# One unit of attention per head: both token tiles in one run of score products, 256-column value products, norm head by head

## The chip, the cores and the metric

The kernel runs on one core of one Trainium2 chip. The metric is the device time of one execution in microseconds, lower is better; the time shown is the median of 3 runs. Engines are called TensorE (PE, with its weight loads as PEld), VectorE (DVE), ScalarE (ACT), GpSimd (POOL) and SyncE (SP).

## The reference

Two layers of a decoder trunk over 256 tokens of 2048 features, in float32. The attention part that the change touches is, cut to its core:

```python
def _diff_attention(q, k, v, lam, rel_bias):          # 8 heads, 2 maps m, dk 64, dv 128
    ...
        s = jnp.einsum('bqhmd,bkhmd->bhmqk', qb, k) * scale + bias   # bias by distance
        s = jnp.where(dist >= 0, s, NEG)
        p = jax.nn.softmax(s, axis=-1)
        p = p[:, :, 0] - lam * p[:, :, 1]
        return jnp.einsum('bhqk,bkhd->bqhd', p, v)
...
    for l in range(2):
        h = _rmsnorm(x, attn_norm_g[l])
        q, k, v, gate_b, gate_c, conv_in = jnp.split(h @ w_in[l], splits, axis=-1)
        q, k = _rmsnorm(q, q_norm_g[l]), _rmsnorm(k, k_norm_g[l])    # per head and map
        attn = _rmsnorm(_diff_attention(q, k, v, lam, rel_bias), subln_g[l]) * (1 - lam_init)
        conv = gate_b * _short_conv(gate_c * conv_in, conv_w[l])
        x = x + jnp.concatenate([attn, conv], axis=-1) @ w_out[l]
        x = x + jnp.square(relu(_rmsnorm(x, mlp_norm_g[l]) @ w_up[l])) @ w_down[l]
```

## The kernel before

Tokens lie in two tiles of 128 (`t`). Every float32 operand of a large product is split in a high part, rounded to fp32r, and a low part, the rest; a product is the sum of three terms, high by high, high by low and low by high (`TERMS`). Weights come by DMA as `raw` tiles; ScalarE makes the high part `whi` (L289), VectorE the low part `wlo` (L290). There are three buffers each of `whi` and `wlo`, so the making of a weight tile waits until TensorE has read the one three before.

A layer's `mixer` runs, in this order on TensorE: q, k and v for heads 0 to 3 (`linear`, L354), q, k and v for heads 4 to 7, then four pairs of the gate columns gc and ci and four of gb (`linear_t`, L376: per weight tile eight products of 512 columns with `whi` and eight of 256 with `wlo`), then the output projection. `mlp` follows.

TensorE's instructions keep the order in which the code is written (`manual_schedule`); the other engines' are put in an order by the framework's scheduler. Everything that isn't the main stream of products is a generator in `work`; the main products call `work.tick()`, and a generator goes on when as many ticks have passed as it yielded last. A tick in `linear` comes after six products of 512 columns, in `linear_t` after four products. So attention is threaded into the product stream that follows: heads 0 to 3 run beside q, k and v of the second half, heads 4 to 7 beside the first gc and ci columns.

The attention of four heads (`attention`) is eight units, one for each token tile `t` and head `i`, each 4 ticks after the one before (`staggered(..., 4)`). A unit does:

- score products (L518): for each map `m`, three terms with 64 rows into a PSUM bank `sc`, of `W` = 128 columns for the first tile and 256 for the second; VectorE adds the bias and takes the row maximum in one instruction (L521), `nm` (L526) negates it, ScalarE takes the exponential with the row sums (L528), VectorE makes the reciprocal, the factor `c` and the mixed map `p` (L531 to L539); then `yield 9`
- one or two transposes of `p` (`ptp`, L544), split by ScalarE and VectorE into `pT` (L546, L547); then `yield 4`
- the value products (L554): three terms of 128 columns for each block `k` of keys, into the head's quarter of the bank `av`
- with the fourth head of a tile: `av` is copied out as `ao` (L562), squared head by head (L567), GpSimd makes the norm factor `af` in five small operations (L569, L396, L398, L572), VectorE multiplies (`an`, L574); then `yield 9`, four transposes (`atp`, L580) and the split into `cat` (L583, L584), which the output projection reads.

PSUM banks named by `bank` come from a rotation of three; `av` has one bank. The early loads of `w_up` (`uraw`) for the MLP stand in SyncE's queue among the loads of `w_in` and use memory that the attention's temporary tiles leave.

Of the kernel before, what the change touches and what calls it, by code (L numbers as in the profile page):

```python
# [21 lines left out]
NH = 8  # L22
DK = 64
# [5 lines left out]
CH = 512  # L29
# [8 lines left out]
TERMS = ((0, 0), (0, 1), (1, 0))  # L38
# [46 lines left out]
def staggered(pieces, apart):  # L85

    entries = [[i * apart, p] for i, p in enumerate(pieces)]
    while entries:
        for e in list(entries):
            if e[0] <= 0:  # L90
                try:
                    e[0] = max(1, next(e[1]))
                except StopIteration:
                    entries.remove(e)
                    continue
            e[0] -= 1
        if entries:
            yield 1
# [3 lines left out]
def trunk(ctx: ExitStack, tc: tile.TileContext, x, w_in, w_out, conv_w, q_norm_g, k_norm_g,  # L102
          lambda_q1, lambda_k1, lambda_q2, lambda_k2, subln_g, attn_norm_g, mlp_norm_g,
          w_up, w_down, rel_bias, selector, out):
    nc = tc.nc
# [45 lines left out]
    ident = const.tile([P, P], F32, tag="ident", name="ident")  # L151
# [41 lines left out]
    s_gain = const.tile([P, DEPTH], F32, tag="sg", name="s_gain")  # L193
    nlam = const.tile([P, DEPTH], F32, tag="nlam", name="nlam")
# [198 lines left out]
    def rstd_of(ss, n, name, shape):  # L393

        e = small.tile([P, shape], F32, tag="rs_e", name=f"{name}_e")
        nc.gpsimd.tensor_scalar(e, ss, 1.0 / n, EPS, op0=ALU.mult, op1=ALU.add)  # L396
        r = small.tile([P, shape], F32, tag="rs_r", name=f"{name}_r")
        nc.gpsimd.tensor_tensor(r, e, mhalf[:, :shape], op=ALU.pow)  # L398
        return r
# [104 lines left out]
    def attention(l, qT, kT, v, h0, dst, bias, tmp):  # L504

        parts = dst.open()
        avs, r0s = {}, {}

        def unit(t, i):
            W = (t + 1) * P  # L510
            h = h0 + i
            s = tmp.tile([P, 2, S], F32, tag="s", name=f"s{h}_{t}")
            mx = small.tile([P, 2], F32, tag="mx", name=f"mx{h}_{t}")
            su = small.tile([P, 2], F32, tag="su", name=f"su{h}_{t}")
            for m in range(2):
                sc = bank(f"sc{h}_{t}_{m}")
                for n, (a, b) in enumerate(TERMS):
                    nc.tensor.matmul(  # L518
                        sc[:, :W], qT[m * DK:(m + 1) * DK, a, i, t * P:(t + 1) * P],
                        kT[m * DK:(m + 1) * DK, b, i, :W], start=(n == 0), stop=(n == 2))  # L520
                nc.vector.tensor_tensor_reduce(  # L521
                    out=s[:, m, :W], in0=sc[:, :W], in1=bias[:, 2 * h + m, S - W:],
                    op0=ALU.add, op1=ALU.max, scale=1.0, scalar=-3.0e38,
                    accum_out=mx[:, m:m + 1])
            nm = small.tile([P, 2], F32, tag="nm", name=f"nm{h}_{t}")
            nc.vector.tensor_scalar_mul(nm, mx, -1.0)  # L526
            for m in range(2):
                nc.scalar.activation(s[:, m, :W], s[:, m, :W], AF.Exp, bias=nm[:, m:m + 1],  # L528
                                     accum_out=su[:, m:m + 1])
            rc = small.tile([P, 2], F32, tag="rc", name=f"rc{h}_{t}")  # L530
            nc.vector.reciprocal(rc, su)  # L531
            if i == 0:
                r0s[t] = small.tile([P, 4], F32, tag="r0", name=f"r0_{h0}_{t}")
            nc.vector.tensor_copy(r0s[t][:, i:i + 1], rc[:, 0:1])
            c = small.tile([P, 1], F32, tag="c", name=f"c{h}_{t}")
            nc.vector.scalar_tensor_tensor(c, su[:, 0:1], rc[:, 1:2], nlam[:, l:l + 1],
                                           op0=ALU.mult, op1=ALU.mult)
            p = tmp.tile([P, S], F32, tag="p", name=f"p{h}_{t}", bufs=2)
            nc.vector.scalar_tensor_tensor(p[:, :W], s[:, 1, :W], c, s[:, 0, :W],  # L539
                                           op0=ALU.mult, op1=ALU.add)  # L540
            yield 9
            tp = bank(f"ptp{h}_{t}")
            for b in range(t + 1):
                nc.tensor.transpose(tp[:, b * P:(b + 1) * P], p[:, b * P:(b + 1) * P], ident)  # L544
            pT = tmp.tile([P, 2, S], F32R, tag="pT", name=f"pT{h}_{t}", bufs=2)
            nc.scalar.activation(pT[:, 0, :W], tp[:, :W], AF.Copy)  # L546
            nc.vector.tensor_sub(pT[:, 1, :W], tp[:, :W], pT[:, 0, :W].bitcast(F32))  # L547
            yield 4
            if i == 0:
                avs[t] = ps.tile([P, CH], F32, tag="av", name=f"av{h0}_{t}", bufs=1)  # L550
            av = avs[t]
            for k in range(t + 1):
                for n, (a, b) in enumerate(TERMS):
                    nc.tensor.matmul(  # L554
                        av[:, i * P:(i + 1) * P], pT[:, a, k * P:(k + 1) * P],
                        v[:, b, k, i * P:(i + 1) * P],
                        start=(k == 0 and n == 0), stop=(k == t and n == 2))
            if i < 3:
                return
            r0 = r0s[t]  # L560
            ao = wide(f"ao{h0}_{t}")
            nc.scalar.activation(ao, av, AF.Copy)  # L562
            ss = small.tile([P, 4], F32, tag="ams", name=f"ams{h0}_{t}")
            junk = wide(f"asq{h0}_{t}")
            for b in range(4):
                c = slice(b * P, (b + 1) * P)
                nc.scalar.activation(junk[:, c], ao[:, c], AF.Square, accum_out=ss[:, b:b + 1])  # L567
            for _ in range(2):
                nc.gpsimd.tensor_tensor(ss, ss, r0, op=ALU.mult)  # L569
            f = rstd_of(ss, P, f"a{h0}_{t}", 4)  # L570
            f2 = small.tile([P, 4], F32, tag="af2", name=f"af2{h0}_{t}")
            nc.gpsimd.tensor_tensor(f2, f, r0, op=ALU.mult)  # L572
            an = wide(f"an{h0}_{t}")
            nc.vector.tensor_tensor(  # L574
                an.rearrange("p (g d) -> p g d", d=P), ao.rearrange("p (g d) -> p g d", d=P),
                f2.unsqueeze(2).to_broadcast([P, 4, P]), op=ALU.mult)
            yield 9
            tp = bank(f"atp{h0}_{t}")
            for b in range(4):
                nc.tensor.transpose(tp[:, b * P:(b + 1) * P], an[:, b * P:(b + 1) * P], ident)  # L580
            tp3 = tp.rearrange("p (h c) -> p h c", c=P)
            hi = parts[:, 0, :, t * P:(t + 1) * P]
            nc.scalar.activation(hi, tp3, AF.Copy, scale=s_gain[:, l:l + 1])  # L583
            nc.vector.scalar_tensor_tensor(  # L584
                parts[:, 1, :, t * P:(t + 1) * P], tp3, s_gain[:, l:l + 1], hi.bitcast(F32),
                op0=ALU.mult, op1=ALU.subtract)
# [460 lines left out]
```

## Time and profile before

| | |
|---|---|
| median of 3 runs | 2182.87 us (2182.46 to 2184.63) |
| profiled execution, span from first to last instruction | 2182.1 us, 29092 instructions |
| its own time | 2182.1 us: the trace shows nothing beside the span |
| TensorE busy | 2160.6 us (99%), granted clock 1.000 |
| VectorE, ScalarE, GpSimd busy | 1604.6, 1271.9 and 140.6 us |
| DMA | 446.64 MB, mean 205 GB/s |

Times in the profile's rows are microseconds from the start of the span. A group's mean duration on TensorE includes the pipeline's depth, so the pace of products is read from the distance of their starts, not from their durations. On VectorE and ScalarE too an instruction starts somewhat before the recorded end of the one ahead.

### The profile page before, as it was taken

What the parts mean: (1) busy time and instruction counts of PE and PEld (TensorE: products, weight loads), DVE (VectorE), ACT (ScalarE), POOL (GpSimd) and SP (SyncE); (2) the same over time, 40 slices, a digit from 0 to 9 for tenths busy, and PEclk for the clock granted to TensorE, in tenths of its full rate; (3) what the DMA queues carried; (4) which work ended last, traced back from release to release, by engine and by line L of the source; (5) the groups of instructions that cost most, each with busy time, mean ns of one, the idle gap of its engine ahead of it and who ended that gap; (6) DMA issues with size and microseconds to landing.
All of it is one profiled execution on the core that took longest, in us unless ns stands there. A gap on an engine that the chain in (4) does not pass through costs nothing.

```text
span 2182.1 us, 29092 instructions
## 1 busy us (share of the span) xinstructions
PE 2160.6 (99%) x11086; PEld 1831.2 (84%) x11086; DVE 1604.6 (74%) x2229; ACT 1271.9 (58%) x1718; POOL 140.6 (6%) x194
## 2 busy tenths in 40 slices
PE   9999999999999999999999999999999999999999
PEld 7888888888888888888888888888888888888887
DVE  5677655688888888855566776557988888887554
ACT  6456444566666666654454654455666666665443
POOL 3011100000000000100011111000000000001000
PEclk9999999999999999999999999999999999999999
DMA  7555766476666766587565566555776666666774
GB/s 253 175 156 175 219 186 190 155 233 221 217 212 213 219 215 212 189 271 242 180 202 177 161 194 202 184 174 187 225 218 219 212 213 216 218 209 211 246 242 145
DMA packets 292509, 446.64 MB, mean 205 GB/s; under 512 B 10420, under 2 KB 191238, under 8 KB 292369
## 3 DMA queue, kind: packets, MB, share of 16 engines
q1 hardware_dynamic: 285664, 423.66, 62.3%
q0 software_dynamic: 6656, 21.10, 2.5%
q8 instruction: 87, 1.43, 0.3%
q14 instruction: 54, 0.43, 0.1%
q10 hardware_dynamic: 48, 0.02, 0.0%
HBM read 425.84 MB, written 18.90 MB: 204 GB/s over the span
## 4 chain that ended last, share of the span: by engine, by line
PE 92%; DMA 3%; DVE 2%; issue 2%; ACT 1%; POOL 0%; DVEq 0%; ACTq 0%; POOLq 0%
PE upc L827 29%; PE dn L987 15%; PE pr L867 12%; PE o L354 8%; PE gc L376 4%; PE ci L376 4%; PE gb L376 4%; PE v L354 4%; PE k L354 4%; PE q L354 3%; DMA uraw<-in_w_up_dram 1%; PE upw L827 1%; PE sc L518 1%; PE av L554 1%; DMA back<-hid 1%
## 5 line engine op out<-in xcount | busy, mean ns | idle before, releaser
L290 DVE TENSOR_TENSOR wlo<-raw,whi 128x1024 fp32r<-128x1024 f32 (+1 forms) x386 | 474.7, 1232 | 378.9 <-ACT whi L289 377.8
L289 ACT ACTIVATE whi<-raw 128x1024 fp32r<-128x1024 f32 (+1 forms) x386 | 406.1, 1055 | 468.4 <-PE dn L987 167.1
L827 PE MATMUL upc<-nT,uhi 128*128 128x512 f32 x1920 | 477.6, 391 | 0.0
L712 ACT ACTIVATE uhi<-uraw 128x1024 fp32r<-128x1024 f32 x256 | 271.1, 1060 | 286.8 <-PE upc L827 252.8
L827 PEld LDWEIGHTS upc<-nT,uhi 128*128 128x128 f32 x1920 | 352.7, 188 | 68.2
L713 DVE TENSOR_TENSOR ulo<-uraw,uhi 128x1024 fp32r<-128x1024 f32 x256 | 312.5, 1221 | 115.1 <-ACT uhi L712 112.7
L987 PE MATMUL dn<-whi,g 128*128 128x512 f32 x1024 | 316.6, 389 | 0.0
L827 PEld LDWEIGHTS upc<-nT,ulo 128*128 128x128 f32 x1920 | 261.9, 190 | 18.7
L827 PE MATMUL upc<-nT,ulo 128*128 128x256 f32 x1920 | 267.7, 282 | 0.0
L987 PEld LDWEIGHTS dn<-whi,g 128*128 128x128 f32 x1024 | 192.2, 188 | 39.8
L987 PE MATMUL dn<-wlo,g 128*128 128x512 f32 x512 | 199.7, 390 | 1.2 <-DVE wlo L290 1.0
L354 PE MATMUL o<-whi,cat 128*128 128x512 f32 x512 | 159.5, 390 | 0.0
L987 PEld LDWEIGHTS dn<-wlo,g 128*128 128x128 f32 x512 | 96.1, 188 | 22.6 <-DVE wlo L290 2.9
L354 PEld LDWEIGHTS o<-whi,cat 128*128 128x128 f32 x512 | 96.1, 188 | 19.7
L354 PE MATMUL o<-wlo,cat 128*128 128x512 f32 x256 | 99.6, 389 | 0.0
L849 POOL DMA_DIRECT2D hid<-h x64 | 34.9, 545 | 949.6 <-ACT h L848 914.1
L867 PE MATMUL pr<-t13h,f 128*128 128x512 f32 x240 | 93.8, 391 | 0.0
L354 PE MATMUL q<-whi,nT 128*128 128x512 f32 x256 | 85.6, 402 | 2.1 <-ACT whi L289 1.9
L354 PE MATMUL k<-whi,nT 128*128 128x512 f32 x256 | 85.5, 400 | 0.0
L867 PE MATMUL pr<-t24h,f 128*128 128x512 f32 x240 | 84.0, 391 | 0.0
L867 PE MATMUL pr<-b2h,f 128*128 128x512 f32 x240 | 84.0, 391 | 0.0
L354 PE MATMUL v<-whi,nT 128*128 128x512 f32 x256 | 83.4, 396 | 0.0
(332 smaller groups left out, 3437.7 us busy)
## 6 DMA issues: line engine op xcount, KB each, us to landing
uraw<-in_w_up_dram SPq DMA_DIRECT2D x128, 1024.0 KB, 5.8
raw<-in_w_in_dram SPq DMA_DIRECT2D x191, 512.0 KB, 4.0
draw<-in_w_down_dram SPq DMA_DIRECT2D x64, 1024.0 KB, 5.1
raw<-in_w_down_dram SPq DMA_DIRECT2D x64, 1024.0 KB, 5.4
raw<-in_w_out_dram SPq DMA_DIRECT2D x64, 512.0 KB, 3.7
hid<-h POOLq DMA_DIRECT2D x64, 256.0 KB, 4.3
back<-hid SPq DMA_DIRECT2D x32, 512.0 KB, 3.5
rev<-by_dist_d POOLq DMA_DIRECT2D x4, 1024.0 KB, 9.7
```

What stands on the lines that cost most here:

```text
L289: a = nc.scalar.activation(hi[:, k], raw[:, k], AF.Copy)
L290: d = nc.vector.tensor_sub(lo[:, k], raw[:, k], hi[:, k].bitcast(F32))
L354: nc.tensor.matmul(acc[:, t], a.ap[:, pa, k % KG, t * P:(t + 1) * P], (hi, lo)[pw][:, j], start=(k == 0 and n == 0), stop=(k == nk - 1 and ...
L376: nc.tensor.matmul(acc[:, f, 0] if part else acc[:, f], wt[:, k % 4, fs], a.ap[:, 0, k % KG] if part else a.ap[:, :, k % KG], start=(part ...
L518: nc.tensor.matmul(sc[:, :W], qT[m * DK:(m + 1) * DK, a, i, t * P:(t + 1) * P], kT[m * DK:(m + 1) * DK, b, i, :W], start=(n == 0), stop=(n ...
L554: nc.tensor.matmul(av[:, i * P:(i + 1) * P], pT[:, a, k * P:(k + 1) * P], v[:, b, k, i * P:(i + 1) * P], start=(k == 0 and n == 0), stop=( ...
L712: nc.scalar.activation(hi, src, AF.Copy)
L713: nc.vector.tensor_sub(lo, src, hi.bitcast(F32))
L827: nc.tensor.matmul(acc[:, 0] if part else acc, wt[:, k], a.ap[:, 0, k % KG] if part else a.ap[:, :, k % KG], start=(part == 0 and kh == 0 ...
L849: nc.gpsimd.dma_start(hid[i // 2][:, i % 2 * 2 * S:(i % 2 + 1) * 2 * S], u)
L867: nc.tensor.matmul(prods[n], fs[j][:, pa, a], b[pw], start=(j == 0 and m == 0), stop=(stop and m == 2))
L987: nc.tensor.matmul(acc[:, t], f[:, pa, k, t * P:(t + 1) * P], (hi, lo)[pw][:, k % 2], start=(b == 0 and k == 0 and m == 0), stop=(b == NB2 ...
```

## The change

A unit is now a head with both of its token tiles; there are four units in an `attention`, 8 ticks apart. Score columns of both tiles lie side by side: 128 of the first tile and 256 of the second, `SPAN = ((0, P), (P, 3 * P))`, in one bank for each map. The twelve score products are one run, in which the two maps alternate. The small operations between (`nm`, reciprocal, `c`) work on both tiles at once, and the mixed map is written over `s`. The transposes `ptp` are three in a run. For the values, the high part of the weights meets both parts of v in one product of 256 columns, the low part meets the high part of v in one of 128; the two column halves of `av` are added when they are copied out (`low`, `ao`). The norm is made for each head when its value products are done, and its two transposes come 6 ticks later instead of 9.

```diff
+        SPAN = ((0, P), (P, 3 * P))
+        def unit(i):
             h = h0 + i
+            sc = [bank(f"sc{h}_{m}") for m in range(2)]
+            for t, (lo, hi) in enumerate(SPAN):
+                for n, (a, b) in enumerate(TERMS):
+                    for m in range(2):
+                        nc.tensor.matmul(
+                            sc[m][:, lo:hi], qT[m * DK:(m + 1) * DK, a, i, t * P:(t + 1) * P],
+                            kT[m * DK:(m + 1) * DK, b, i, :hi - lo],
+                            start=(n == 0), stop=(n == 2), skip_group_check=True)
             for m in range(2):
-                sc = bank(f"sc{h}_{t}_{m}")
-                for n, (a, b) in enumerate(TERMS):
-                    nc.tensor.matmul(
-                        sc[:, :W], qT[m * DK:(m + 1) * DK, a, i, t * P:(t + 1) * P],
-                        kT[m * DK:(m + 1) * DK, b, i, :W], start=(n == 0), stop=(n == 2))
...
             yield 9
-            for b in range(t + 1):
+            for b in range(3):
                 nc.tensor.transpose(tp[:, b * P:(b + 1) * P], p[:, b * P:(b + 1) * P], ident)
...
             yield 4
-            for k in range(t + 1):
-                for n, (a, b) in enumerate(TERMS):
-                    nc.tensor.matmul(
-                        av[:, i * P:(i + 1) * P], pT[:, a, k * P:(k + 1) * P],
-                        v[:, b, k, i * P:(i + 1) * P],
-                        start=(k == 0 and n == 0), stop=(k == t and n == 2))
-            if i < 3:
-                return
...
+            av = ps.tile([P, NT, 2, P], F32, tag="av", name=f"av{h}", bufs=1)
+            cols = slice(i * P, (i + 1) * P)
+            for t in range(NT):
+                for part in range(2):
+                    for k in range(t + 1):
+                        nc.tensor.matmul(
+                            av[:, t, 0] if part else av[:, t],
+                            pT[:, part, (t + k) * P:(t + k + 1) * P],
+                            v[:, 0, k, cols] if part else v[:, :, k, cols],
+                            start=(part == 0 and k == 0), stop=(part == 1 and k == t),
+                            skip_group_check=True)
+            both = wide(f"ao{h}").rearrange("p (a t c) -> p a t c", a=2, t=NT)
+            low, ao = both[:, 0], both[:, 1]
+            nc.scalar.activation(low, av[:, :, 1], AF.Copy)
+            nc.vector.tensor_add(ao, av[:, :, 0], low)
+            ss = small.tile([P, NT], F32, tag="ams", name=f"ams{h}")
+            for t in range(NT):
+                nc.scalar.activation(low[:, t], ao[:, t], AF.Square, accum_out=ss[:, t:t + 1])
...
-            yield 9
+            nc.vector.tensor_tensor(ao, ao, f2.unsqueeze(2).to_broadcast([P, NT, P]), op=ALU.mult)
+            yield 6
...
-        yield from staggered([unit(t, i) for t in range(NT) for i in range(4)], 4)
+        yield from staggered([unit(i) for i in range(4)], 8)
```

How instructions move is shown at two places beside gc and ci of the first layer. First TensorE, before: from the last score products to the transposes of the normalized heads of the first tile (`atp_0`, which read `an_0`).

```order
L518 MATMUL sc_1_0_2095<-kT_1433,qT_1096 128x256 x3
L518 MATMUL sc_1_1_2100<-kT_1433,qT_1096 128x256 x3
L376 MATMUL ci_1891<-nT_3_355,wlo 128x256 x4
L554 MATMUL av_1_2120<-v_1672,pT_1_2071 128x128 x6
L544 MATMUL ptp_1_2127<-ident,p_1_1987 128x128 x2
L376 MATMUL gc_2145<-nT_0_162,whi 128x512 x8
L376 MATMUL gc_2145<-nT_0_162,wlo 128x256 x8
L554 MATMUL av_1_2120<-v_1672,pT_1_2130 128x128 x6
L544 MATMUL ptp_1_2174<-ident,p_1_2041 128x128 x2
L376 MATMUL gc_2145<-nT_1_222,whi 128x512 x4
L580 MATMUL atp_0_2190<-ident,an_0_2066 128x128 x4
```

TensorE, after, at head 6: `sc_0_1839` and `sc_1_1840` are the scores of head 6, `ptp_1873` the transposes of head 5, `atp_1894` those of the normalized head 4 (`ao_1797`), `av_1907` the values of head 5.

```order
L518 MATMUL sc_0_1839<-kT_1398,qT_1080 128x256
L518 MATMUL sc_1_1840<-kT_1398,qT_1080 128x256
L376 MATMUL ci_1817<-nT_0_162,wlo 128x256 x4
L547 MATMUL ptp_1873<-ident,s_1724 128x128 x3
L376 MATMUL ci_1817<-nT_1_222,whi 128x512 x8
L579 MATMUL atp_1894<-ident,ao_1797 128x128 x2
L376 MATMUL ci_1817<-nT_1_222,wlo 128x256 x8
L557 MATMUL av_1907<-v_1621,pT_1877 128x256
L557 MATMUL av_1907<-v_1621,pT_1877 128x128
L557 MATMUL av_1907<-v_1621,pT_1877 128x256 x2
L557 MATMUL av_1907<-v_1621,pT_1877 128x128 x2
```

Final transposes now stand once for each head, twelve main products behind a score run; before, they stood once for each token tile and 24 main products, two runs of value products and two of `ptp` behind the last score run. The two maps' score products, three and three before, alternate.

Second VectorE, before: around the multiply that makes `an_0`.

```order
L526 TENSOR_SCALAR nm_1_2105<-mx_1_2093 128x2
L539 SCALAR_TENSOR_TENSOR p_1_2041<-s_1_2019,c_1_2039 128x256
L290 TENSOR_TENSOR wlo<-raw,whi 128x1024
L574 TENSOR_TENSOR an_0_2066<-ao_0_2050,af_0_2064 128x512
L531 RECIPROCAL rc_1_2109<-su_1_2094 128x2
L390 TENSOR_TENSOR ci00w<-ci_1891,ci00l 128x512
L547 TENSOR_TENSOR pT_1_2130<-ptp_1_2127,pT_1_2130 128x256
```

VectorE, after: the last score reduction of head 6 (`s_1836`) and the multiply of head 4 (`ao_1797`).

```order
L524 ISA s_1836,mx_1837<-sc_1_1840,bias 128x256
L524 ISA mx_1837 128x1
L290 TENSOR_TENSOR wlo<-raw,whi 128x1024
L530 TENSOR_SCALAR nm_1857<-mx_1837 128x4
L550 TENSOR_TENSOR pT_1877<-ptp_1873,pT_1877 128x384
L575 TENSOR_TENSOR ao_1797<-ao_1797,af_1809 128x256
L536 RECIPROCAL rc_1863<-su_1838 128x4
L538 SCALAR_TENSOR_TENSOR c_1865<-su_1838,nlam,rc_1863 128x2
L542 SCALAR_TENSOR_TENSOR s_1836<-s_1836,c_1865 128x128
L542 SCALAR_TENSOR_TENSOR s_1836<-s_1836,c_1865 128x256
```

The multiply that the final transposes read, one for each token tile before, is now one for each head, and stands behind the score reductions of the head two later, a `wlo`, `nm` and the `pT` of the head between. On ScalarE the squares of head 7 (`ams_2119`) stand between two weight tiles:

```order
L581 ACTIVATE cat_1646<-atp_2096,s_gain 128x256
L565 ACTIVATE ao_2116<-av_2109 128x256
L289 ACTIVATE whi<-raw 128x1024
L569 ACTIVATE ao_2116,ams_2119<-ao_2116 128x128 x2
L289 ACTIVATE whi<-raw 128x1024
```

Before, the four squares of the second tile stood directly behind the copy of `av`; now a `whi` is between.

More of the change, by code (lines that the diff above doesn't have):

```diff
@@ L526, in unit @@
             nc.vector.tensor_scalar_mul(nm, mx, -1.0)
             for m in range(2):
-                nc.scalar.activation(s[:, m, :W], s[:, m, :W], AF.Exp, bias=nm[:, m:m + 1],
-                                     accum_out=su[:, m:m + 1])
-            rc = small.tile([P, 2], F32, tag="rc", name=f"rc{h}_{t}")
+                for t, (lo, hi) in enumerate(SPAN):
+                    nc.scalar.activation(s[:, m, lo:hi], s[:, m, lo:hi], AF.Exp,
+                                         bias=nm[:, m, t:t + 1], accum_out=su[:, m, t:t + 1])
@@ L531, in unit @@
+            rc = small.tile([P, 2, NT], F32, tag="rc", name=f"rc{h}")
             nc.vector.reciprocal(rc, su)
[L532 to L536, printed above, removed]
+            c = small.tile([P, NT], F32, tag="c", name=f"c{h}")
@@ new lines, in unit @@
+            f = rstd_of(ss, P, f"a{h}", NT)
+            f2 = small.tile([P, NT], F32, tag="af2", name=f"af2{h}")
+            nc.gpsimd.tensor_tensor(f2, f, rc[:, 0], op=ALU.mult)
+            nc.vector.tensor_tensor(ao, ao, f2.unsqueeze(2).to_broadcast([P, NT, P]), op=ALU.mult)
+            yield 6
+            tp = bank(f"atp{h}")
+            for t in range(NT):
+                nc.tensor.transpose(tp[:, t * P:(t + 1) * P], ao[:, t], ident)
+            hi = parts[:, 0, i]
+            nc.scalar.activation(hi, tp[:, :S], AF.Copy, scale=s_gain[:, l:l + 1])
```

65 lines of the change are left out of this document (21 added, 44 removed).

## The prediction

> **What bounds the kernel now.** I read the page first, then the waits of TensorE, then the timelines of the two places where attention runs. TensorE does 92% of the chain that ended last and is busy all through:
>
> ```profile
> PE 2160.6 (99%) x11086; PEld 1831.2 (84%) x11086; DVE 1604.6 (74%) x2229; ACT 1271.9 (58%) x1718; POOL 140.6 (6%) x194
> PE 92%; DMA 3%; DVE 2%; issue 2%; ACT 1%; POOL 0%; DVEq 0%; ACTq 0%; POOLq 0%
> PE pr L867 <- DVE f L859: 3.2, 4, 1.0
> ```
>
> The third row is the longest of TensorE's waits; of that view's twelve rows none is on an attention product (L518, L544, L554, L580). So attention costs what its products take in TensorE's stream, and the change is worth what it takes out of that stream, less any wait it brings.
>
> What a run of products takes I measure from the start of the last 512-column product before it to the start of the second one behind it, less two ordinary steps of 0.23 us (138.70 to 138.93 below). Columns: start, us, engine, line, operands, count.
>
> ```profile
> 102.56 0.39 PE L354 MATMUL q<-whi,nT 128*128 128x512 f32 x1
> 102.88 0.56 PE L518 MATMUL sc<-kT,qT 64*128 64x128 f32 x6
> 103.36 0.50 PE L354 MATMUL q<-whi,nT 128*128 128x512 f32 x1
> 103.70 0.40 PE L354 MATMUL q<-wlo,nT 128*128 128x512 f32 x1
> ```
> ```profile
> 122.15 0.39 PE L354 MATMUL k<-whi,nT 128*128 128x512 f32 x1
> 122.47 0.62 PE L518 MATMUL sc<-kT,qT 64*128 64x256 f32 x6
> 123.02 0.50 PE L354 MATMUL k<-whi,nT 128*128 128x512 f32 x1
> 123.36 0.40 PE L354 MATMUL k<-wlo,nT 128*128 128x512 f32 x1
> ```
> ```profile
> 138.70 0.39 PE L354 MATMUL k<-whi,nT 128*128 128x512 f32 x1
> 138.93 0.78 PE L554 MATMUL av<-v,pT 128*128 128x128 f32 x6
> 139.55 0.41 PE L544 MATMUL ptp<-ident,p 128*128 128x128 f32 x2
> 139.71 0.48 PE L354 MATMUL v<-whi,nT 128*128 128x512 f32 x1
> 140.02 0.39 PE L354 MATMUL v<-wlo,nT 128*128 128x512 f32 x1
> ```
>
> Scores of a first tile take 1.14 - 0.46 = 0.68 us, of a second tile 1.21 - 0.46 = 0.75; six value products and two transposes 1.32 - 0.46 = 0.86, or 0.11 each.
>
> **Score products.** The twelve of a head (2 layers x 8 heads = 16 heads) become one run. The first product of a run starts 0.32 after its forerunner instead of 0.23, and the second product behind it comes 0.34 after the first: about 0.2 us per run goes for entering and leaving products of 64 rows. Within, six 128-column products pass in 0.48 (102.88 to 103.36), drain included, where six value products need 0.62 (138.93 to 139.55). So the two halves of 64 rows already overlap, though their instructions stand three and three. Three more pairs in the longer run, at 0.11 a pair, give 0.75 + 0.33 = 1.08 against 0.68 + 0.75 = 1.43: 0.35 less per head, 5.6 us in all. From below: if they went one by one, six more cost 0.66 and only 0.02 is left (0.3 us in all). I take 5.6, since the rows show six in less than six steps.
>
> Here a rule speaks otherwise. The Trainium skill ("TensorE: Matmul & The Clock Gate", Part 2) says that products stay in program order and only weight loads are pulled ahead. By it the old three-and-three order could not pair, and the new alternation would be the first to do so; that is a rival below. The skill's "TensorEngine Tiling (Array Packing)" (Tiling Modes) says that changing the tiling mode drains the engine; the 0.32 and 0.34 agree.
>
> **Value products.** A head had nine of 128 columns; now three of 256 (the high weights against both parts of v) and three of 128. The pace of 256 columns is in the second stage:
>
> ```profile
> 198.59 1.12 PE L376 MATMUL gc<-nT,wlo 128*128 128x256 f32 x8
> 199.54 0.86 PE L554 MATMUL av<-v,pT 128*128 128x128 f32 x6
> ```
>
> 0.95 / 8 = 0.12. So 9 x 0.11 = 0.99 becomes 3 x 0.12 + 3 x 0.11 = 0.69: 0.30 less per head, 4.8 us in all. Bounds: 3 us if the strided two-part operand runs slower (0.16 each), 5.3 at 0.11 each. The same skill page (Back-to-back issue gap) prices an isolated product at N / 2.4 + 2.5 ns; by that formula, an estimate, 128 columns cost 56 ns and 256 cost 109, and the value products would gain nothing. The trace's 0.11 and 0.12 decide. Transposes keep their number (three and two per head): nothing.
>
> So 10.4 us leave TensorE's stream. The new evictions, additions and small GpSimd operations lie on engines that are not the bound. In SyncE's queue the third early load of w_up now stands ahead of two loads of w_in that it followed, and it waits for the attention's buffers:
>
> ```profile
> raw<-in_w_in_dram SPq DMA_DIRECT2D x191, 512.0 KB, 4.0
> ```
>
> A w_in load lands in 4.0 us, and the two are used some six weight tiles of 2.8 us later (8 x 0.23 + 8 x 0.12): hidden; if that cover were gone, a tile or 2.8 us a layer. What can cost is an order in which TensorE waits.
>
> **Beside q, k and v (heads 0 to 3 of each layer): no wait.** Between a head's last score product and the final transposes two heads back now lie 18 products of 512 columns, 4.1 us, and VectorE has the multiply ready by then (worked out below). I take nothing; up to 0.5 us a head if the q/k norms get in between, 4 us in all.
>
> **Beside gc and ci (heads 4 to 7): a wait at the final transposes.** The distance there is short. The old order shows the pieces:
>
> ```profile
> 183.28 0.74 PE L376 MATMUL ci<-nT,wlo 128*128 128x256 f32 x4
> 183.86 0.45 PE L554 MATMUL av<-v,pT 128*128 128x128 f32 x3
> 184.14 0.29 PE L544 MATMUL ptp<-ident,p 128*128 128x128 f32 x1
> 184.19 2.11 PE L376 MATMUL ci<-nT,whi 128*128 128x512 f32 x8
> 186.14 0.64 PE L376 MATMUL ci<-nT,wlo 128*128 128x256 f32 x4
> ```
>
> In the new order four products of 256 (0.58, 183.28 to 183.86), three transposes (3 x 0.11) and eight products of 512 (1.95, 184.19 to 186.14) stand between the end of a score run and the transposes of the head two back: 2.85 us. In that time VectorE must do, in its fixed order, four score reductions, a wlo, nm, pT and then the multiply that these transposes read:
>
> ```profile
> 175.82 0.29 DVE L521 CUSTOM_DVE_ANT_0 s<-sc,bias 128x128 f32<-128x128 f32 x1 [0.52 <-PE sc L518]
> 176.04 0.09 DVE L521 DVE_READ_ACCUMULATOR2_ANT mx<- 128x1 f32 x1
> ```
> ```profile
> 184.31 0.42 DVE L521 CUSTOM_DVE_ANT_0 s<-sc,bias 128x256 f32<-128x256 f32 x1
> 184.66 0.08 DVE L521 DVE_READ_ACCUMULATOR2_ANT mx<- 128x1 f32 x1
> 184.66 1.22 DVE L290 TENSOR_TENSOR wlo<-raw,whi 128x1024 fp32r<-128x1024 f32 x1
> 185.80 0.16 DVE L526 TENSOR_SCALAR nm<-mx 128x2 f32<-128x2 f32 x1
> 185.87 0.28 DVE L547 TENSOR_TENSOR pT<-ptp,pT 128x128 fp32r<-128x128 f32 x1
> ```
> ```profile
> 193.80 0.41 DVE L547 TENSOR_TENSOR pT<-ptp,pT 128x256 fp32r<-128x256 f32 x1
> ```
>
> By starts: 2 x 0.22 + 2 x 0.35 + 1.14 + 0.07 = 2.35; pT of 384 columns about 0.5 (0.28 and 0.41 less one overhead); the multiply of 256 columns 0.41; about 0.2 for the handovers: 3.45. The transposes come 0.6 us late at a head that meets only this. It is head 5. The others meet a longer chain, through ScalarE's squares and GpSimd:
>
> ```profile
> 193.03 0.32 ACT L567 ACTIVATE asq<-ao 128x128 f32<-128x128 f32 x1
> 193.23 0.20 ACT L567 ACTIVATION_READ_ACCUMULATOR asq<-ao 128x1 f32 x1
> 193.32 0.31 ACT L567 ACTIVATE asq<-ao 128x128 f32<-128x128 f32 x1
> ```
> ```profile
> 206.61 1.06 ACT L289 ACTIVATE whi<-raw 128x1024 fp32r<-128x1024 f32 x1 [1.41 <-PE gc L376]
> ```
> ```profile
> 36.30 0.72 POOL L398 TENSOR_TENSOR row_r<-row_e,mhalf 128x2 f32<-128x2 f32 x1
> ```
> ```profile
> 194.38 0.47 POOL L569 TENSOR_TENSOR ams<-ams,r 128x4 f32<-128x4 f32 x2 [10.96 <-ACT asq L567]
> ```
> ```profile
> 195.22 1.01 POOL L398 TENSOR_TENSOR a_r<-a_e,mhalf 128x4 f32<-128x4 f32 x1
> 196.31 0.25 POOL L572 TENSOR_TENSOR af<-a_r,r 128x4 f32<-128x4 f32 x1
> ```
>
> A square takes 0.29 to the next one (193.03 to 193.32), two take 0.6. GpSimd takes 2.18 for four columns (194.38 to 196.56), so 1.9 for two, with the power at 0.72 instead of 1.01. ScalarE's order puts a whi ahead of the squares of each head, and a whi waits for TensorE to have read an older one (the row at 206.61). For head 7: from the end of its value products TensorE does 8 x 512, 8 x 256, 8 x 512, 1.95 + 0.95 + 1.85 = 4.75, up to the transposes; the whi can start after the first eight, 2.15, and then 1.0 for it, 0.6 for the squares, 1.9 for GpSimd, 0.4 for the multiply and 0.25 of handovers make 6.3: 1.55 late. Head 6 has three more transposes in that distance (5.05): 1.25 late. At head 4 the product of gc with rowb stands ahead in GpSimd's queue and I put 1.0. Together 0.6 + 1.0 + 1.25 + 1.55 = 4.4 us a layer, 8.8 in all. Bounds: 2.4 us in all if every transpose waits 0.3 only, 17.6 if each waits 2.2. While TensorE waits, all its later products are queued behind, and the wait is lost in full.
>
> **Sum.** 2182.1 - 5.6 - 4.8 + 8.8 = 2180.5 us for the profiled execution. Its span lies 0.8 below the median of the runs shown, so 2181.3 there: 1.6 us less, which is within the 0.2% (4.4 us) that a measurement of this kernel can tell from no change.
>
> **Rivals.** (1) Faster: the waits beside gc and ci stay small, 0.3 each, 2.4 us. Then -10.4 + 2.4 = -8.0, or 2174.9 us beside the median of 2182.9. For it: TensorE waits for no attention step now. Against: the order fixes the multiply behind a wlo and pT, 3.45 against 2.85. It decides below 0.75 us a head. Chance 0.2.
>
> (2) Faster by the alternation: the old runs did not pair, twelve products alone would go in six steps, about 6 x 0.11 = 0.66 plus the 0.2 of entry and exit, 0.86 instead of 1.43: 0.57 x 16 = 9.1 instead of 5.6, and with my waits 2181.3 - 3.5 = 2177.8 us, 5.1 less than now. This is what the program-order rule of the Trainium skill's page on TensorE would do here. Against: the 0.48 for six. Chance 0.08.
>
> (3) Slower: the finish of a head becomes a chain in series at all eight heads beside gc and ci, each squares-GpSimd-multiply chain starting only when TensorE has released a whi and ending 2.2 us late. 17.6 - 10.4 = +7.2: 2190.1 us. For it: head 7 already comes to 1.55, and the yield before the transposes is 6 ticks instead of 9. Against: at heads 4 and 5 a score run and a product tile more lie in between. It decides from (10.4 + 4.4) / 8 = 1.85 us a head. Chance 0.22.
>
> **How the numbers follow.** The forecast case, within 0.2%, has the remaining 0.5. Faster 0.28 is rivals 1 and 2, slower 0.22 is rival 3. The range goes from 2174 (rival 1 with the best value products) to 2190 (rival 3) and leaves out about 2 in 10, the outer parts of both.
>
> **What would show it.** TensorE's score group (12 products) near 1.08 us a run; value runs near 0.7; a new row in TensorE's waits, the final transposes on VectorE's normalized product, eight times, some 4 to 14 us in total and only beside gc and ci. No such row makes the forecast wrong to the fast side; the same row with 2 us each, or waits on wlo or whi in that stage, to the slow side.

## Result, and the profile after

The changed kernel takes 2205.24 us (median of 4 runs, 2204.23 to 2206.73), the kernel before 2183.75 us beside it (4 runs, 2182.46 to 2186.62): ratio 1.0097, 95% interval 1.0085 to 1.0109. It is slower by 21.5 us, where 1.6 us less was forecast, and it lies above the range. The profiled spans are 2203.6 and 2182.1 us, also 21.5 apart.

The page's first part, busy time of each engine:

```profile
PE 2166.5 (98%) x11038; PEld 1825.3 (83%) x11038; DVE 1597.3 (72%) x2165; ACT 1272.6 (58%) x1718; POOL 157.7 (7%) x234
```

TensorE's idle time (span less busy time) goes from 21.5 to 37.1 us, 15.6 more. Its busy time grows too, by 5.9 us, though some 10 us of attention products were to leave it. Two things to look for, then: new waits, and products that became slower.

**The runs that were rewritten cost what was forecast.** TensorE's timeline around a score run and around a value run (start, us, engine, line, operands, count):

```profile
101.95 0.39 PE L354 MATMUL q<-whi,nT 128*128 128x512 f32 x1
102.27 0.95 PE L518 MATMUL sc<-kT,qT 64*128 64x128 f32 x12
...
103.49 0.40 PE L354 MATMUL q<-wlo,nT 128*128 128x512 f32 x1
```
```profile
139.43 0.40 PE L354 MATMUL k<-whi,nT 128*128 128x512 f32 x1
139.66 0.80 PE L557 MATMUL av<-v,pT 128*128 128x256 f32 x6
...
140.58 0.39 PE L354 MATMUL v<-wlo,nT 128*128 128x512 f32 x1
```

By the prediction's own measure the score run takes 1.54 - 0.46 = 1.08 us (forecast 1.08) and the value run 1.15 - 0.46 = 0.69 (forecast 0.69).

**New waits.** TensorE's waits, the rows on attention and on the q and k norms (total us, times, longest). None of them is in the view of before:

```profile
PE atp L579 <- DVE ao L575: 12.5, 8, 1.8
...
PE q01tp L496 <- DVE q01n L487: 1.5, 1, 1.5
PE q11tp L496 <- DVE q11n L487: 1.4, 1, 1.4
...
PE k11tp L496 <- DVE k11n L487: 0.7, 1, 0.7
PE k01tp L496 <- DVE k01n L487: 0.7, 1, 0.7
```

The eight waits at the final transposes are the forecast ones, at 12.5 us instead of 8.8. The four others, 4.3 us, are at transposes that the prediction put no wait at: those of the second half's q and k norms.

**Slower products far from the change.** The o stage (L354) and the dn stage (L985 now, L987 before) are not in the diff. TensorE in the same 80 us of the o stage, before and then after (busy time, products started, granted clock, DMA share, GB/s):

```profile
320.00:400.00 80.00, 80.00 (x366) 1.00 0.53 159
```
```profile
320.00:400.00 80.00, 80.00 (x358) 1.00 0.55 168
```

The clock is full and TensorE never idle in both, yet 8 matmuls fewer pass, 2.2%. (Some of them are transposes; the rest are o's products.) The same by line, for 1024 of dn's 1536 products, before and after (busy us, mean ns of one):

```profile
L987 PE MATMUL dn<-whi,g 128*128 128x512 f32 x1024 | 316.6, 389 | 0.0
```
```profile
L985 PE MATMUL dn<-whi,g 128*128 128x512 f32 x1024 | 321.9, 395 | 0.0
```

Products overlap, so the mean of one is longer than a step; from start to start the median goes from 227 to 232 ns (means 226.8 and 232.4, steps over 300 ns left out) in both stages. With 768 products of o and 1536 of dn I took 2304 x 0.0054 = 12.4 us; the steps of both stages, added up, are 12.3 us longer. The products of q, k, v, gc, ci, gb and up keep their pace within 0.5 ns.

So: 10.4 us saved; 12.5 + 4.3 us of new waits and 12.4 us of slower products; 18.8 of the 21.5 us. Of the other 2.7 us most is no work of the change: for a few microseconds beside ci of the second layer the granted clock was below full, where it is 1.00 in the same window of before (same columns as above):

```profile
1278.00:1284.00 6.00, 5.84 (x28) 0.72 0.40 137
```

6.00 x (1 - 0.72) = 1.7 us, an estimate. Why it fell there no run shows; other executions have such stretches at other places. The remaining 1.0 us was not taken apart in full; 0.5 of it is a third stage of slower products, which comes below.

### The profile page after: what moved, and what is told of

Same layout as the page of the kernel before. It is cut to its first block, busy times and chain, and to the rows that moved or that the text cites. A ratio compares the mean times of both kernels' runs of the same rounds, so it can differ in the third digit from the quotient of the medians.

```text
span 2203.6 us, 28981 instructions
## 1 busy us (share of the span) xinstructions
PE 2166.5 (98%) x11038; PEld 1825.3 (83%) x11038; DVE 1597.3 (72%) x2165; ACT 1272.6 (58%) x1718; POOL 157.7 (7%) x234
## 4 chain that ended last, share of the span: by engine, by line
PE 87%; DVE 4%; DMA 3%; issue 2%; POOL 2%; ACT 1%; DVEq 0%; POOLq 0%; ACTq 0%
PE upc L825 28%; PE dn L985 16%; PE pr L865 12%; PE o L354 8%; PE gb L376 4%; PE ci L376 4%; PE k L354 4%; PE gc L376 3%; PE q L354 3%; PE v L354 3%; DMA uraw<-in_w_up_dram 2%; PE upw L825 1%; DVE ulo L711 1%; DVE wlo L290 1%; PE sc L518 1%
## 5 line engine op out<-in xcount | busy, mean ns | idle before, releaser
L985 PE MATMUL dn<-whi,g 128*128 128x512 f32 x1024 | 321.9, 395 | 0.0
L985 PEld LDWEIGHTS dn<-whi,g 128*128 128x128 f32 x1024 | 192.8, 188 | 44.8
L985 PE MATMUL dn<-wlo,g 128*128 128x512 f32 x512 | 202.4, 395 | 0.7 <-DVE wlo L290 0.6
L354 PE MATMUL o<-whi,cat 128*128 128x512 f32 x512 | 162.3, 395 | 0.0
L985 PEld LDWEIGHTS dn<-wlo,g 128*128 128x128 f32 x512 | 96.4, 188 | 24.8 <-DVE wlo L290 2.4
L354 PEld LDWEIGHTS o<-whi,cat 128*128 128x128 f32 x512 | 96.5, 188 | 22.1
L354 PE MATMUL o<-wlo,cat 128*128 128x512 f32 x256 | 101.0, 394 | 0.0
L354 PE MATMUL q<-whi,nT 128*128 128x512 f32 x256 | 84.0, 397 | 2.8 <-ACT whi L289 2.7
L354 PE MATMUL k<-whi,nT 128*128 128x512 f32 x256 | 85.3, 399 | 0.0
L354 PE MATMUL v<-whi,nT 128*128 128x512 f32 x256 | 83.4, 396 | 0.0
```

Of the source, the lines that this page charges most:

```text
L354: nc.tensor.matmul(acc[:, t], a.ap[:, pa, k % KG, t * P:(t + 1) * P], (hi, lo)[pw][:, j], start=(k == 0 and n == 0), stop=(k == nk - 1 and ...
L985: nc.tensor.matmul(acc[:, t], f[:, pa, k, t * P:(t + 1) * P], (hi, lo)[pw][:, k % 2], start=(b == 0 and k == 0 and m == 0), stop=(b == NB2 ...
```

## Experiments

What could change the pace of products that nobody touched? The change drops the tag `r0` (four buffers of 32 bytes) from the pool `small`, so every pool opened behind it starts 128 bytes lower in a partition. Addresses, as the built kernels have them, are given here modulo 256 bytes. nT, whi and wlo, which lie ahead of it, stand at 96 in both kernels; cat, g and raw lie behind it: 96 before, 224 after. The theory: an o or dn product is slower because its two operands (cat or g, and whi or wlo) are now 128 apart. The rival: the new order or the new load on the other engines slows it.

| run | what it is | median us | before beside it | ratio (95%) |
|---|---|---|---|---|
| e1_pad_after | changed kernel, 128 bytes back in `small` | 2190.68 | 2183.88 | 1.0032 (1.0020 to 1.0045) |
| e2_pad_before | kernel before, 128 bytes more in `small` | 2198.21 | 2183.88 | 1.0066 (1.0054 to 1.0079) |
| e3_late_transpose | e1, final transposes after 9 ticks | 2179.17 | 2183.88 | 0.9980 (0.9971 to 0.9989) |
| e4_three_and_three | e1, score products three and three | 2192.20 | 2183.88 | 1.0039 (1.0027 to 1.0052) |
| e5_const_shift | changed kernel, 128 bytes more ahead of all | 2207.79 | 2185.53 | 1.0100 (1.0087 to 1.0114) |
| e6_shift64 | changed kernel, 64 bytes more in `small` | 2201.88 | 2185.53 | 1.0077 (1.0063 to 1.0090) |
| e7_shift32 | changed kernel, 32 bytes more in `small` | 2212.87 | 2185.53 | 1.0123 (1.0107 to 1.0138) |
| e8_nine_values | e1, nine value products of 128 | 2191.70 | 2185.53 | 1.0031 (1.0019 to 1.0043) |
| e9_late_qk | e3, norms' transposes after 10 ticks | 2175.53 | 2184.24 | 0.9963 (0.9950 to 0.9975) |
| e10_all_late | e9, final transposes after 11 ticks | 2173.65 | 2184.24 | 0.9954 (0.9941 to 0.9968) |
| e11_operands_apart | changed kernel, only the pools of cat and of g moved back | 2192.74 | 2184.93 | 1.0033 (1.0020 to 1.0045) |
| e12_sources_apart | changed kernel, all behind `small` but these two pools moved back | 2205.61 | 2184.93 | 1.0092 (1.0078 to 1.0106) |

**The addresses, in both orders.** In the changed kernel (e1), and with the same idea in the kernel before (e2):

```diff
-            c = small.tile([P, NT], F32, tag="c", name=f"c{h}")
+            c = small.tile([P, 16], F32, tag="c", name=f"c{h}")[:, :NT]
```
```diff
-            c = small.tile([P, 1], F32, tag="c", name=f"c{h}_{t}")
+            c = small.tile([P, 16], F32, tag="c", name=f"c{h}_{t}")[:, :1]
```

> The changed kernel with 128 bytes more in the pool `small`, so that every tile behind that pool lies at the address that it had before; nothing else. Address theory (the changed kernel runs its 2304 products of the o and dn stages at 232 ns instead of 227 because cat and g, the operands that are read there, moved by 128 bytes): they return to 227 ns, 2304 x 0.0054 = 12.4 us less than the changed kernel, 2192.8 us. Rival (the slower pace comes from the new order or from the new engine load, not from where tiles lie): 232 ns stays, 2205 us.

> The kernel before with 128 bytes more in the pool `small`, so that cat, g and all behind it lie where the changed kernel has them; the order of the instructions is the old one. Address theory: the products of o and dn go from 227 to 232 ns, 2183.7 + 12.4 = 2196 us. Rival: 227 ns stays, 2183.7 us.

dn's products by line, in e1 and then in e2:

```profile
L985 PE MATMUL dn<-whi,g 128*128 128x512 f32 x1024 | 316.1, 389 | 0.0
```
```profile
L987 PE MATMUL dn<-whi,g 128*128 128x512 f32 x1024 | 322.2, 395 | 0.0
```

The bytes alone switch it, whatever the order of the instructions: 389 in e1 as before the change, 395 in e2 as after it. From start to start the o and dn products stand at 227 ns in e1 and 232 in e2. The kernel before slows by 14.3 us of median (span 2182.1 to 2194.2, 12.1 more); the changed one gains 1.0097 - 1.0032 = 0.65%, 14 us. The rival is out.

**Which place matters?** e5 moves everything by 128, so the operands stay 128 apart but trade places:

```diff
-    mhalf = const.tile([P, NH], F32, tag="mhalf", name="mhalf")
+    mhalf = const.tile([P, NH + 32], F32, tag="mhalf", name="mhalf")
```

> The changed kernel with 128 bytes more in the first pool, `const`: now every tile moves up by 128 bytes. Taken modulo 256, nT, whi and wlo go from 96 to 224 and cat and g from 224 to 96; their distance stays 128. Theory of the distance (a product is slower where its stationary and its moving operand lie 128 apart): o and dn stay at 232 ns, q, k, v and up at 227, 2205 us. Theory of the place (a stationary operand at 224 is read slower): o and dn return to 227 ns, q, k and v (1152 products), gc, ci and gb and up go to 232, 2210 us or more.

o and dn stay at 232 ns and q, k, v and up at 227: the distance counts, not the place. e11 and e12 ask whose distance. raw, from which ScalarE and VectorE make whi and wlo while TensorE works, had moved together with cat and g. e11 puts the following in front of the pool of cat, and the like in front of that of g; e12 has it together with e1's edit:

```diff
+            gapb = scope.enter_context(tc.tile_pool(name="gapb", bufs=1)).tile(
+                [P, 32], F32, tag="gapb", name="gapb")
+            nc.gpsimd.memset(gapb, 0.0)
             bpool = scope.enter_context(tc.tile_pool(name="bpool", bufs=8))
```

> The changed kernel with 128 bytes put in front of the pools of cat and of g alone: modulo 256, cat and g lie at 96 again, as whi and wlo do; raw, from which whi and wlo are made, stays at 224. Theory of the operands (what matters is the distance of the product's own two operands): o and dn return to 227 ns, 2190.7 us. Theory of the sources (what matters is the distance between what ScalarE and VectorE read, raw, and what TensorE reads): 232 ns, 2205 us.

> The other half: 128 bytes more in `small`, which brings raw back to 96, and 128 bytes in front of cat and g, which puts these at 224 as in the changed kernel. Theory of the operands: 232 ns, 2205 us. Theory of the sources: 227 ns, 2190.7 us.

dn in e11, and in e12, each with a third stage, the last products pr of the MLP:

```profile
L991 PE MATMUL dn<-whi,g 128*128 128x512 f32 x1024 | 316.6, 389 | 0.0
L957 PE MATMUL pr<-whi,f 128*128 128x512 f32 x64 | 20.4, 395 | 0.0
```
```profile
L991 PE MATMUL dn<-whi,g 128*128 128x512 f32 x1024 | 322.4, 395 | 0.0
L957 PE MATMUL pr<-whi,f 128*128 128x512 f32 x64 | 20.1, 390 | 0.0
```

Both came out as the theory of the operands has it, in the rows and in the medians (2192.74 and 2205.61). The pr rows are a check inside the same executions. f lies behind `small` but in neither of the two pools: in e11 it stays 128 from whi, in e12 it is back at whi's place, and pr goes the other way than dn. From start to start these 64 products have a mean of 227.2 ns before and in e1, 232.9 in the changed kernel and in e11, 233.0 in e2, 233.3 in e5 and 227.6 in e12, as the distance has it each time.

So the products are slower where what TensorE holds as its stationary operand and what it streams lie 128 bytes apart instead of 0. By what mechanism no run shows, and no run moved them by a whole 256, so the period itself isn't tested.

**How the price runs with the distance.**

```diff
-            self.r = small.tile([P, NT], F32, tag="rowf", name="rowf", bufs=2)
+            self.r = small.tile([P, 16], F32, tag="rowf", name="rowf", bufs=2)[:, :NT]
```
```diff
-            self.across = small.tile([P, 2, S], F32, tag="rowb", name="rowb", bufs=1)
+            self.across = small.tile([P, 2 * S + 8], F32, tag="rowb", name="rowb", bufs=1)[
+                :, :2 * S].rearrange("p (a s) -> p a s", a=2)
```

> The changed kernel with 64 bytes more in the pool `small`: modulo 256, cat and g lie at 32, whi and wlo at 96, 64 apart instead of 128 (the changed kernel) or 0 (the kernel before). Theory that only equal places are fast: 232 ns, 2205 us. Theory that only a distance of 128 is slow: 227 ns, 2191 us, as with 128 bytes. A price that grows with the distance would give some 229.5 ns, 2198 us.

> The changed kernel with 32 bytes more behind the pool `small`'s largest tile: modulo 256, cat and g lie at 0, whi and wlo at 96. Theory that only equal places are fast: 232 ns, 2205 us. Theory that only a distance of 128 is slow: 227 ns, 2191 us. A price that grows with the distance: 231 ns, 2201 us.

e6 (operands 64 apart), and e7 (96 apart), by line:

```profile
L825 PE MATMUL upc<-nT,uhi 128*128 128x512 f32 x1920 | 481.1, 392 | 0.0
L985 PE MATMUL dn<-whi,g 128*128 128x512 f32 x1024 | 320.0, 393 | 0.0
L985 PE MATMUL dn<-wlo,g 128*128 128x512 f32 x512 | 199.3, 389 | 1.1 <-DVE wlo L290 0.9
```
```profile
L826 PE MATMUL upc<-nT,uhi 128*128 128x512 f32 x1920 | 481.7, 393 | 0.0
L986 PE MATMUL dn<-whi,g 128*128 128x512 f32 x1024 | 322.2, 395 | 0.0
```

From start to start, all dn products together have a mean of 226.8 ns at distance 0, 228.9 at 64, 233.3 at 96 and 232.4 at 128, so the price does not run in a straight line. And here the theory is not the whole story. whi and wlo lie at the same distance from g, yet at 64 the products with whi take 230.3 ns and those with wlo 226.2, no more than at 0; at 96 it is 232.7 and 234.6. And the up products, whose operands nT and uhi still lie at equal places, go from 228.4 to 230.4 (e6) and 230.6 ns (e7), 1920 x 0.002 = 4 us; the larger part of what e7 is slower by than the changed kernel. In both runs raw and all else behind `small` moved with cat and g. So these two runs show that a smaller shift costs time too, not what each distance of the operands costs by itself; the cause of the rest stays open.

**The waits at the final transposes.**

```diff
-            yield 6
+            yield 9
             tp = bank(f"atp{h}")
```

> The kernel with the 128 bytes more, and the final transposes of a head 9 ticks instead of 6 behind its value products. Theory (the transposes wait because the distance is too short for the chain of squares, GpSimd and the multiply): the waits at atp, 12.5 us, and their refill, 1.7 us, go: with the addresses of before 2192.8 - 14.2 = 2178.6 us, which is under the kernel before. Rival (something else is late next in the place of atp, a buffer or a weight that is split later): a new wait of 5 us or more, 2184 us or above.

TensorE's waits in e3:

```profile
PE atp L579 <- DVE ao L575: 3.0, 2, 1.5
...
PE q01tp L496 <- DVE q01n L487: 1.4, 1, 1.4
PE q11tp L496 <- DVE q11n L487: 1.4, 1, 1.4
...
PE k01tp L496 <- DVE k01n L487: 0.8, 1, 0.8
```

At atp six of the eight waits go, 9.4 us of e1's 12.4; head 7 keeps its 1.5 us a layer. The spans of e1 and e3 lie 9.7 us apart, the ratios 0.52%, 11 us, with an interval of some 3 us either way. No wait took the place. The kernel is now faster than the one before, by 0.2%.

**The order of the score products.**

```diff
-                for n, (a, b) in enumerate(TERMS):
-                    for m in range(2):
+                for m in range(2):
+                    for n, (a, b) in enumerate(TERMS):
```

> The kernel with the 128 bytes more, and the score products of a tile written three of one map, then three of the other, instead of in turns. Theory (products of 64 rows of the two halves overlap in either order): the run of twelve stays at 1.08 us and the time is that of the kernel with the 128 bytes alone, 2192.8 us. Rival (only products that alternate overlap): a run of twelve grows to some 1.4 us, 16 x 0.35 = 5.6 us more, 2198 us.

```profile
101.56 0.39 PE L354 MATMUL q<-whi,nT 128*128 128x512 f32 x1
101.88 0.96 PE L518 MATMUL sc<-kT,qT 64*128 64x128 f32 x12
...
103.11 0.39 PE L354 MATMUL q<-wlo,nT 128*128 128x512 f32 x1
```

1.55 - 0.46 = 1.09 against 1.08 in turns: the order makes no difference, and rival (2) of the prediction, which needed 0.86, falls. What it does not show is why: that the halves overlap in any order, as I had it, or that a product of 64 rows is short by itself. The program-order rule of the Trainium skill ("TensorE: Matmul & The Clock Gate", Part 2) fits only the second reading; no run here separates the two.

**What the 256-column products are worth.**

```diff
-                for part in range(2):
-                    for k in range(t + 1):
+                for k in range(t + 1):
+                    for part, b in ((0, 0), (0, 1), (1, 0)):
                         nc.tensor.matmul(
-                            av[:, t, 0] if part else av[:, t],
-                            pT[:, part, (t + k) * P:(t + k + 1) * P],
-                            v[:, 0, k, cols] if part else v[:, :, k, cols],
+                            av[:, t, b], pT[:, part, (t + k) * P:(t + k + 1) * P],
+                            v[:, b, k, cols],
```

The two column blocks of v start their sums apart here, and part of the sum is lost, so this kernel's values are not those of the reference; number and form of the products are as said.

> The kernel with 128 bytes more in `small`, and each 256-column value product written as two of 128: nine of 128 per head as before the change, in one run, and everything behind them as changed. Theory (a product pair of 128 costs 0.11 + 0.11 and one of 256 only 0.12): a run grows from 0.70 to 0.99 us, 16 x 0.29 = 4.7 us more than with the 128 bytes alone, 2190.7 + 4.7 = 2195.4 us. Rival (the time of columns alone counts, so 256 columns cost as much as 2 x 128): 2190.7 us.

TensorE's timeline and its waits in e8:

```profile
141.16 0.39 PE L354 MATMUL k<-whi,nT 128*128 128x512 f32 x1
141.38 1.12 PE L557 MATMUL av<-v,pT 128*128 128x128 f32 x9
...
142.62 0.39 PE L354 MATMUL v<-wlo,nT 128*128 128x512 f32 x1
```
```profile
PE atp L578 <- DVE ao L574: 7.6, 6, 1.5
```

The run takes 1.46 - 0.46 = 1.00 us instead of 0.69, 5.0 us over the 16 heads as expected, and yet the time is that of e1 (1.0031 against 1.0032; the two intervals together leave some 4 us either way). The wait at atp went from 12.4 to 7.6 us, and the stretch from the first q product to the first gb product takes 516.5 us in both layers together, in e1 517.0. TensorE came later to transposes that were not ready anyway. The saving of the value products is real, and as the change stands it is spent in the wait behind it: the theory had the products right and the time wrong, the rival the time right for a wrong reason.

**The waits of the norms, and the last one.**

```diff
             out_.append(qn)
-        yield 8
+        yield 10
```
```diff
-            yield 9
+            yield 11
             tp = bank(f"atp{h}")
```

> The kernel with the 128 bytes more and the final transposes after 9 ticks, and besides the transposes of the q and k norms after 10 ticks instead of 8. Theory (VectorE's lump of four score reductions delays the norms' multiplies of the second half, and TensorE meets that at q01tp, q11tp, k01tp and k11tp): these waits, 4.3 us in all, go, 2179.2 - 4.3 = 2174.9 us. Rival (the wait moves on to the first score products or to whatever VectorE has to do next): 2178 us or more.

> As the run with the norms at 10 ticks, and the final transposes after 11 ticks instead of 9. Theory (head 7's transposes, 1.5 us late a layer at 9 ticks, come after their multiply at 11): 2174.9 - 3.0 - 0.4 of refill = 2171.5 us. Rival (the later transposes fall behind another VectorE step and wait there): 2175 us or more.

TensorE's waits in e9, and in e10:

```profile
PE atp L579 <- DVE ao L575: 2.9, 2, 1.5
...
PE q11tp L496 <- DVE qT L500: 0.4, 1, 0.4
PE q01tp L496 <- DVE qT L500: 0.4, 1, 0.4
```
```profile
PE sc L518 <- DVE qT L500: 1.6, 2, 0.8
```

In e9 the norms' waits go from 3.6 us (e3) to 0.8, and the time with them. In e10 head 7's wait goes too, but 1.6 us come back at the score runs of head 3, which now stop until VectorE has done qT, the step that reads the q norm's transposes: a wait of the rival's kind, though not at the place that it named. The two kernels can't be told apart by their times (spans 2171.7 and 2171.9). e10 has the lowest median, 10.6 us below the kernel before in its runs, with some 3 us either way: near the 10.4 us of the prediction's first two terms, once the addresses are restored and nearly every new wait is gone.

## Why the prediction was wrong

**Score and value products: right**, each to 0.01 us a head, and so is 10.4 us in all.

**The base of the sum: wrong, the largest term.** The sum started from 2182.1 us and changed only what the diff changes. It held without a word that 2304 products of o and dn keep their 227 ns. They went to 232: 12.4 us, in no term, bound or rival. Without it the time would have been that of e1, 2190.7, just above the range; with the waits as measured the prediction's own sum, 2182.1 - 10.4 + 12.5 + 4.3 = 2188.5 us, comes to 0.7 of e1's span, 2187.8.

**Beside q, k and v: "I take nothing" failed.** It was 4.3 us, near the bound of 4, but at another place. The bound was for final transposes that the q and k norms make late, and these did not wait at all: the eight waits at atp are all beside gc and ci. What waited was the transposes of the norms, made late by the new attention steps; no term of the sum had them. VectorE before the transposes of the second half's q norm, then GpSimd and TensorE there:

```profile
121.86 0.74 DVE L542 SCALAR_TENSOR_TENSOR s<-s,c 128x128 f32<-128x128 f32 x2
122.52 0.68 DVE L481 TENSOR_REDUCE q01ms<-q01sq 128x8 f32<-128x512 f32 x1
...
125.14 1.23 DVE L290 TENSOR_TENSOR wlo<-raw,whi 128x1024 fp32r<-128x1024 f32 x1 [0.42 <-ACT whi L289]
...
126.42 0.74 DVE L500 SCALAR_TENSOR_TENSOR qT<-q01tp,q_gain,qT 128x512 fp32r<-128x512 f32 x1
127.08 0.68 DVE L487 TENSOR_TENSOR q01n<-q,q01f 128x512 f32<-128x512 f32 x1
```
```profile
124.47 1.64 POOL L398 TENSOR_TENSOR q_r<-q_e,mhalf 128x8 f32<-128x8 f32 x1
```
```profile
127.91 0.63 PE L496 MATMUL q01tp<-ident,q01n 128*128 128x128 f32 x4 [1.45 <-DVE q01n L487]
```

The norm's sum of squares stands behind both multiplies of a head. GpSimd, which turns it into a factor (q_r), is done at 126.11, and a wlo, which itself waits for ScalarE, holds VectorE until 126.37; then comes the qT of the other token tile and only then the norm's multiply. I had followed only the attention's own multiply through that order. (My expectation of e9 put the delay on the four score reductions; these rows put it on the multiplies, GpSimd, wlo and qT. That later transposes remove the wait holds for either, and no run parts their shares.)

**Beside gc and ci: right in kind, too small.** The waits per layer, heads 4 to 7, were 1.84, 0.87, 1.82 and 1.74 us against 1.0, 0.6, 1.25 and 1.55. Head 4 on GpSimd, on VectorE and on TensorE:

```profile
183.31 1.30 POOL L662 TENSOR_TENSOR gc00w<-gc00w,rowb 128x512 f32<-128x512 f32 x1 [23.63 <-PE sc L518]
184.57 1.44 POOL L571 TENSOR_TENSOR ams<-ams,rc 128x2 f32<-128x2 f32 x2
...
187.15 0.19 POOL L574 TENSOR_TENSOR af<-a_r,rc 128x2 f32<-128x2 f32 x1
```
```profile
184.32 1.36 DVE L290 TENSOR_TENSOR wlo<-raw,whi 128x1024 fp32r<-128x1024 f32 x1
```
```profile
187.86 0.44 PE L579 MATMUL atp<-ident,ao 128*128 128x128 f32 x2 [1.84 <-DVE ao L575]
```

The product with rowb stands ahead on GpSimd, as foreseen. But GpSimd's chain takes 187.34 - 184.57 = 2.77 us where the prediction put 1.9. The 1.9 is about right for a chain that nothing disturbs, as one beside q, k and v shows, 130.71 - 128.90 = 1.81 us:

```profile
128.90 0.47 POOL L571 TENSOR_TENSOR ams<-ams,rc 128x2 f32<-128x2 f32 x2 [2.79 <-ACT ao L569]
...
130.51 0.20 POOL L574 TENSOR_TENSOR af<-a_r,rc 128x2 f32<-128x2 f32 x1
```

Beside gc and ci each head's chain has a step that starts while VectorE makes a wlo. At head 4 the two first operations take 1.44 us instead of 0.47. Head 7 on GpSimd and on VectorE:

```profile
211.34 0.93 POOL L571 TENSOR_TENSOR ams<-ams,rc 128x2 f32<-128x2 f32 x2 [0.79 <-ACT ao L569]
...
213.40 0.19 POOL L574 TENSOR_TENSOR af<-a_r,rc 128x2 f32<-128x2 f32 x1
```
```profile
210.72 1.22 DVE L290 TENSOR_TENSOR wlo<-raw,whi 128x1024 fp32r<-128x1024 f32 x1 [1.27 <-ACT whi L289]
```

Here they take 0.93, and the chain 2.25; at heads 5 and 6 the chain takes 2.80 and 2.58. In all sixteen chains of this trace the steps that start beside a wlo are longer, and they end with it or later; steps that meet only a qT or a kT, which reads one operand from PSUM, keep their 0.19 to 0.70 us. So the term that was too small is GpSimd's 1.9 us: it left out what VectorE does beside it. Head 5 was to meet only VectorE's order; there too VectorE stood ready and waited 0.32 us for GpSimd's factor. The Trainium skill's "SBUF — State Buffer" (Who interferes with whom) says that a VectorE instruction with two SBUF inputs contends with a GpSimd instruction that reads SBUF; these rows agree, the wlo at head 4 too being longer (1.36) than its usual 1.22, but no run was made for it.

**The rivals.** Rival (1) is refuted by the waits, rival (2) by the run of twelve at 1.08 us and by e4. Rival (3) has the right sign for a wrong reason: its eight waits were to be 2.2 us each and to decide from 1.85 up; they are 1.56 in the mean, and with them alone the sum is -10.4 + 12.5 = +2.1 us, no change that a measurement tells.

## What to carry to other kernels

A change that adds or drops a buffer moves every pool behind it: compare the addresses, and in the trace the pace of products that the diff doesn't touch, before any other account. A saving on the engine that sets the end is lost, as in e8, while the next thing it meets isn't ready: move the meeting first (two numbers of ticks here), then count the saving. And when following whether a result will be ready, follow every stream in that engine's order, not only the one that the diff edits.

## What the hardware showed

A move of one operand of a product by 128 bytes against the other changed its pace: 227 ns from start to start at equal places (modulo 256), 232 to 233 at 128 apart, for 512 columns at a granted clock of 1.00, in the o, dn and last pr stages alike, in both orders of instructions. The Trainium skill ("TensorE: Matmul & The Clock Gate", Step-by-step: what each phase is for) says that loading the next weights doesn't take read bandwidth from the running product, since the two have read ports of their own. It gives no reason to expect the 5 ns a product by which e11 and e12 differ, and the measurement decides; whether the loads cause them, no run shows. What a distance of 64 or 96 costs by itself, and why the up products slow at those shifts though their own operands did not move apart, is open.

On GpSimd two operations on 128x2 that take 0.47 us together took 0.93 and 1.44 us when the first started while VectorE subtracted two tiles in SBUF (`wlo`, 1.22 and 1.36 us).
